# Five edits to the instruction order of a hybrid decoder layer: ffn1's last differences, a pair sum, residual loads, the memory's keys and the end of attention

## The chip, the cores and the metric

The kernel runs on one core of one Trainium2 chip. The metric is the device time of one execution in microseconds (us); before the change it is 2645.61 us, the median of 3 runs (2640.96 to 2645.98). The core's engines work side by side, each through its own queue in order: TensorE (PE: matmuls, with PEld for its weight loads), VectorE (DVE), ScalarE (ACT), GpSimd (POOL) and SyncE (SP). SP, POOL and ACT issue DMAs from their queues too.

## What is computed

One decoder layer over 1024 tokens of width 1024, all in float32, cut to its frame:

```python
def swiglu(h, w_gu, w_down):
    g, u = jnp.split(h @ w_gu, 2, axis=-1)          # D_FF = 2816
    return (jax.nn.silu(g) * u) @ w_down

f = swiglu(rmsnorm(h, ffn1_pre_g), ffn1_w_gu, ffn1_w_down)
h = h + 0.5 * rmsnorm(f, ffn1_post_g)
m = hybrid_mixer(rmsnorm(h, mix_pre_g), ...)        # stick-breaking attention | Mamba-2 SSD, then @ w_out
h = h + rmsnorm(m, mix_post_g)
c = memory_cross_attention(rmsnorm(h, xa_pre_g), rmsnorm(mem, mem_g), wq, wkv, wo)   # 256 memory rows
h = h + rmsnorm(c, xa_post_g)
f = swiglu(rmsnorm(h, ffn2_pre_g), ffn2_w_gu, ffn2_w_down)
return h + 0.5 * rmsnorm(f, ffn2_post_g)
```

## The kernel before

**Precision.** Every product of float32 values is made of three matmuls in a rounded float32 format: `split` (L263 to L269) casts a tile to its high part on ACT (L266) and subtracts that on DVE to get the low part (L268); `mm3` then multiplies high by high, high by low and low by high. A "product" below is 12 matmuls of 128x512, or 24 for a whole depth of 1024. In names, `xh` and `xl`, `whi` and `wlo`, `ath` and `atl`, `ohi` and `olo` are such pairs of parts.

**Order.** PE's instructions are chained in the order in which the program writes them. A planner's clock (`self.clock`, in planned nanoseconds of PE) counts their costs, and work for the other engines is put into `self.later` with a due time: `at(t, f)` runs `f` when the clock has passed `t`, so that its instructions are written between the matmuls of that moment. `run_later(inf)` runs all that is left at once. `urgent()` gives an instruction a higher priority, so that it may stand ahead of others on its engine. `merge(a, ta, b, tb)` runs two generators beside each other so that each has used the same share of its planned time `ta` or `tb`. On each engine the result is one queue; what stands in it behind a waiting instruction waits too.

**The first feed-forward (ffn1).** Its up projection (`up_phase` with `begin`) computes a few tiles plainly for both token halves, and the others with seven products in place of eight (`seven`, L786): a 2 by 2 block scheme, in which the two token halves and the two halves of the depth form the blocks of the activations, and sums and differences of blocks are multiplied with sums and differences of weight blocks. `S[1]`, `S[4]`, `S[5]`, `B11`, `B12`, `B21`, `B22` are such activation blocks of four tiles (k = 0 to 3) in high and low part. `B12` holds the differences gain x b - d of the second half's tiles b and d. `again(k)` (L717) loads b and d by POOL's queue, `scale` (L677) multiplies d by its gain on ACT, and `last(k)` (L720) makes the difference on DVE (L690) and splits it. `below(k)` (L711) does the same for `B21`. `homes` (L841) names the tiles in which b and d lie: the tiles `braw`, `rpost` and `dg`, `acc0` and `acc1` for k = 0 to 2; k = 3 uses a `blk`, a buffer of the weight blocks. The weight blocks themselves are made by POOL (`wc`, L741) and split into `whi`/`wlo` or `blk`.

In `seven`, a = x B22 is copied to SBUF by ACT (L795), b = x B21 likewise (L799), POOL subtracts (L800), DVE adds the product c of S[1] (L805, the tile `e`), then that of S[4] (L809); the bank of a then takes the product by B12 on top, and that of c, freed by L805, the product by S[5].

**The second feed-forward (ffn2)** does the same with `begin` false. Behind each odd tile, `pair_sums` (L637) forms sums of two tiles (`cb`, L643 on DVE), which ACT's queue stores (L645) for the down projection.

**The residual.** `resid(hh, step, start)` (L376) puts eight loads on POOL's queue, `step` apart. In the first down projection, `finish` (L949) calls it at m == 3, and at m == 4 calls `run_later(inf)`.

**Keys of the memory** (`keys`, L1479): eight products of 24 matmuls of 128x256; DVE evicts each into `sq0` (L1491), `split` puts pairs into a tile `Bt`, and SP stores a pair (L1498). DVE's additions into `yacc` (L1454) belong to the state-space branch.

**The end of attention.** `units(p)` makes the scores of head pair p (sigmoid on ACT, L1746, a scan on DVE, L1750), transposes them and multiplies them with the values; a head's sum goes to a mix tensor in DRAM through POOL (L1767). The last pair's work, `tail`, is merged with `beside`: the first output products (`mix_first`, six of eight output tiles) and the values of the memory (`memory_values`, eight products of 24 matmuls of 128x256, evicted into `ev`, transposed, split into `vo` and stored by SP, L1866). Then `mix_out` loads the mix tensors: SP loads a row into one of four buffers `oraw` (L1946), ACT squares it (L1938, L1941) and casts it (L273), DVE adds the square to `asum` (L1942) and makes the low part (L275); PE needs `asum` for the norm in the midst of the first output products.

Of the kernel before, what the change touches and what calls it, by code (L numbers as in the profile page):

```python
# [47 lines left out]
class Kern:  # L48
# [512 lines left out]
    def up_phase(self, sp, sp2, wgu, gpre, act_d, bank, load, plain, sizes, rw=None, begin=None):  # L561
# [75 lines left out]
        def pair_sums(f, even, odd):  # L637

            (t0, t1), (u0, u1) = even, odd
            j, c = f // 2, self.clock  # L640
# [6 lines left out]
            def fresh(n, a, b, op):  # L647
                combine(n, self.t(ftp, [P, H], F32, "cb", bufs=3), a, b, op)

            fresh("s6", t1, t0, ALU.subtract)  # L650
# [25 lines left out]
        def scale(x, d):  # L676
            self.kp(nc.scalar.activation(x, x, AF.Copy, scale=self.par(gpre, d)))  # L677
# [42 lines left out]
        def last(k):  # L720
            b, d = tmp["bd", k]
            if not begin:
                scale(d, k + 4)
            combine(B12[k], b, k, d, ALU.subtract)

        def at(t, f, *args):
            self.later.append((t, lambda: f(*args)))
# [114 lines left out]
        if begin:  # L842
            for k, x in enumerate((
                [(rw, "braw", 2)] * 2, [(rw, "rpost"), (self.tp, "dg")], [(rw, "acc0"), (rw, "acc1")],
            )):
                homes["ca", k] = homes["bd", k] = x
# [17 lines left out]
        if begin:  # L864
# [10 lines left out]
            for hh in range(2):  # L875
                if hh:
                    for k in range(4):
                        at(self.clock + 500 + 3000 * k, below, k)
                        if k < 3:
                            at(self.clock + 3000 + 3000 * k, again, k)  # L880
                            at(self.clock + 12000 + 1000 * k, lambda k=k: scale(tmp["bd", k][1], k + 4))
# [25 lines left out]
        for k in range(4):  # L907

            if k == 3 and begin:
                at(self.clock + 200, again, k)  # L910
                at(self.clock + 3500, lambda: scale(tmp["bd", 3][1], 7))
            at(self.clock + (1200 * k if begin else 1500 * k + 500), last, k)
# [20 lines left out]
    def down1(self, sp, wdn, act_d, xs_d, gpost, gnext):  # L933
# [15 lines left out]
        def finish(m, i):  # L949
            if m == 3:  # L950
# [3 lines left out]
                self.resid(0, 2000, 16000)  # L954
# [234 lines left out]
    def ssd(self, close):  # L1189

        nc, ap = self.nc, self.ap
        with self.tc.tile_pool(name=self.nm("ssa"), bufs=1, reuse_waits="tile") as ep, \
# [286 lines left out]
            def keys(n0, n1):  # L1479
# [6 lines left out]
                for n in range(n0, n1):  # L1486
# [4 lines left out]
                    nc.vector.tensor_tensor(out=t, in0=ps, in1=rm, op=ALU.mult)  # L1491
                    i = n % 2
                    if i == 0:
                        env["ko"] = self.t(sp, [P, 4, MEM], F32R, "Bt")
                    o = env["ko"]
                    self.split(o[:, i, :], o[:, 2 + i, :], t)
                    if i == 1:
                        nc.sync.dma_start(out=self.kv_d[n // 2][0].bitcast(F32), in_=o.bitcast(F32))  # L1498
# [78 lines left out]
    def attention(self):  # L1577
        nc, ap = self.nc, self.ap
        with self.pools("at", ["o", "a"], ["w"]) as (op, sp, wsp, pp):
# [310 lines left out]
            self.merge(tail(), 26000, beside(), 21000 + 5200 * MIXED)  # L1890
# [470 lines left out]
```

## Time and profile before

| | us |
|---|---|
| median of 3 runs | 2645.61 |
| the runs | 2640.96, 2645.61, 2645.98 |
| the profiled execution | 2636.52 |
| its span, first to last instruction | 2634.7 |
| PE busy | 2587.8 |
| mean granted PE clock | 0.994 |

The profile is of one execution. A row of the timeline gives the start, the duration, the engine with the line and the operation, output<-input, and in brackets the idle time before it and who ended it. A matmul of 128x512 in a row of them is shown with 0.39 us, but the next starts 0.23 us after it: they are pipelined. A row with x12 stands for twelve.

### The profile page before, as it was taken

How to read it: one execution, taken by the hardware profiler on the slowest of the kernel's cores; microseconds unless marked ns; L12 is line 12 of the kernel's file. 1: busy time of each engine (PE TensorE's matmuls, PEld its weight loads, DVE VectorE, ACT ScalarE, POOL GpSimd, SP SyncE). 2: the span in 40 equal slices, each digit the busy share in tenths (PEclk: the TensorE clock that was granted, in tenths of full speed). 3: DMA queues.
4: the chain of work that ended last, by engine and by line, in shares of the span. 5: the costliest groups of instructions: out<-in, count | busy, mean ns of one | idle time of the engine just before them, and what ended most of it. 6: DMA issues, size and time to landing. Idle time of an engine off the chain costs nothing. (4 is left out here: it accounts for less than half of the span.)

```text
span 2634.7 us, 36858 instructions
## 1 busy us (share of the span) xinstructions
PE 2587.8 (98%) x12850; PEld 2155.5 (82%) x12850; DVE 1981.6 (75%) x3044; ACT 1292.3 (49%) x2300; POOL 599.4 (23%) x713
## 2 busy tenths in 40 slices
PE   9899999999999999999999999999999999999999
PEld 7688888778777778888888897888878788888887
DVE  6778887778779775777777777767556888777777
ACT  7434444545356563555555555345544433333553
POOL 2555553110100000111111110101011555452000
PEclk9999999999999999999999999999999999999999
DMA  6558888875655226655555556547558453326554
GB/s 221 170 183 286 278 272 292 279 246 182 240 184 177 81 73 196 173 149 148 141 147 132 170 153 229 192 149 249 197 185 295 140 176 116 100 97 227 188 171 152
DMA packets 212970, 489.82 MB, mean 186 GB/s; under 512 B 26544, under 2 KB 35120, under 8 KB 212784
## 3 DMA queue, kind: packets, MB, share of 16 engines
q1 hardware_dynamic: 163472, 371.58, 42.8%
q0 software_dynamic: 25984, 73.42, 9.2%
q10 hardware_dynamic: 23328, 42.48, 4.3%
q8 instruction: 101, 1.65, 0.3%
q14 instruction: 85, 0.70, 0.1%
HBM read 327.46 MB, written 138.94 MB: 177 GB/s over the span
## 5 line engine op out<-in xcount | busy, mean ns | idle before, releaser
L139 PE MATMUL mm<-xh,whi 128*128 128x512 f32 x1320 | 522.6, 405 | 7.4 <-ACT xh L273 3.0
L139 PE MATMUL mm<-xl,whi 128*128 128x512 f32 (+1 forms) x1252 | 488.1, 390 | 4.7 <-DVE xl L268 4.4
L139 PE MATMUL mm<-xh,wlo 128*128 128x512 f32 x1272 | 489.0, 392 | 0.0
L139 PEld LDWEIGHTS mm<-xh,whi 128*128 128x128 f32 x1320 | 249.1, 189 | 50.3 <-ACT xh L266 3.9
L139 PEld LDWEIGHTS mm<-xh,wlo 128*128 128x128 f32 x1272 | 238.9, 188 | 52.0 <-DVE wlo L268 0.2
L139 PEld LDWEIGHTS mm<-xl,whi 128*128 128x128 f32 x1252 | 236.6, 189 | 39.3 <-DVE xl L268 6.3
L1750 DVE TENSOR_TENSOR_SCAN nb<-nb,begin 128x128 f32<-128x128 f32 (+7 forms) x128 | 171.5, 1352 | 52.4 <-ACT nb L1746 51.9
L1746 ACT ACTIVATE nb<-z,scale 128x128 f32<-128x128 f32 (+2 forms) x192 | 107.7, 580 | 77.8 <-PE z L139 77.5
L268 DVE TENSOR_TENSOR wlo<-wraw,whi 128x1024 fp32r<-128x1024 f32 x70 | 85.4, 1221 | 54.8 <-ACT whi L266 51.4
L266 ACT CAST whi<-wraw 128x1024 fp32r<-128x1024 f32 (+1 forms) x87 | 83.8, 964 | 79.2 <-PE mm L139 55.2
L1767 POOL DMA_DIRECT2D mix<-sq x64 | 52.9, 826 | 229.1 <-DVE sq L1765 131.0
L658 ACT ACTIVATE ft<-ft 128x512 f32<-128x512 f32 x88 | 55.5, 632 | 98.1 <-DVE ft L657 96.1
L139 PE MATMUL dn<-xh,wlo 128*128 128x512 f32 x296 | 101.3, 390 | 0.0
L741 POOL TENSOR_TENSOR wc<-wraw,raw 128x512 f32<-128x512 f32 x56 | 80.3, 1433 | 64.7 <-DVE whi L268 17.8
L741 POOL TENSOR_TENSOR wc<-raw,wraw 128x512 f32<-128x512 f32 x55 | 81.1, 1474 | 51.0 <-DVE blk L268 21.6
L268 DVE TENSOR_TENSOR atl<-tr,ath 128x512 fp32r<-128x512 f32 (+1 forms) x108 | 67.9, 632 | 29.9 <-ACT ath L266 29.5
L826 POOL TENSOR_TENSOR ft<-ft,e 128x512 f32<-128x512 f32 x37 | 59.7, 1613 | 121.1 <-DVE e L825 45.1
L139 PE MATMUL mm<-ath,v 128*128 128x256 f32 x320 | 86.1, 292 | 0.1
L266 ACT CAST ath<-tr 128x512 fp32r<-128x512 f32 (+1 forms) x108 | 58.8, 546 | 55.5 <-PE tr L142 50.9
L139 PE MATMUL dn<-xh,blk 128*128 128x512 f32 x264 | 85.2, 389 | 0.0
L266 ACT CAST wlo<-wc 128x512 fp32r<-128x512 f32 x79 | 49.1, 621 | 71.0 <-PE dn L139 26.1
L139 PE MATMUL mm<-atl,v 128*128 128x256 f32 x320 | 83.1, 282 | 0.7 <-DVE atl L268 0.7
(566 smaller groups left out, 6799.7 us busy)
## 6 DMA issues: line engine op xcount, KB each, us to landing
whi<-dwhi SPq DMA_DIRECT2D x82, 512.0 KB, 3.6
wlo<-dwlo SPq DMA_DIRECT2D x82, 512.0 KB, 4.7
wraw<-in_w_gu SPq DMA_DIRECT2D x43, 512.0 KB, 4.1
raw<-in_w_gu SPq DMA_DIRECT2D x37, 512.0 KB, 4.2
dwhi<-bh SPq DMA_DIRECT2D x66, 256.0 KB, 4.1
dwlo<-bl SPq DMA_DIRECT2D x66, 256.0 KB, 4.3
wraw<-xs SPq DMA_DIRECT2D x56, 256.0 KB, 3.1
xs<-ft ACTq DMA_DIRECT2D x54, 256.0 KB, 3.3
```

Of the source, the lines that this page charges most:

```text
L139: self._pe(self.nc.tensor.matmul(out, lhsT, rhs, start=start, stop=stop, skip_group_check=self.more), cost)
L266: self.kp(self.nc.scalar.copy(hi, src))
L268: self.nc.vector.tensor_tensor(out=lo, in0=src, in1=hi.bitcast(F32), op=ALU.subtract)
L658: nc.scalar.activation(t, t, AF.Silu)
L741: nc.gpsimd.tensor_tensor(out=t, in0=a, in1=b, op=op)
L826: nc.gpsimd.tensor_tensor(out=t1, in0=t1, in1=e, op=ALU.mult)
L1746: nc.scalar.activation(nb[:, s0:s1], z[:, 0:n], AF.Sigmoid, scale=sc[:, i : i + 1])
L1750: nc.vector.tensor_tensor_scan(out=nb[:, 0:Wd][:, ::-1], data0=nb[:, 0:Wd][:, ::-1], data1=begin[:, S - Wd : S][:, ::-1], initial=0.0, op0 ...
L1767: nc.gpsimd.dma_start(out=self.mix_d[p][a * 64 : a * 64 + 64, csl], in_=o, accum_op=ALU.add)
```

## The change

Five places are edited, and nothing that is computed changes.

1. ffn1's last differences. k = 3 gets two `cb` tiles as its home. `below` is due every 2200 instead of every 3000, `again` now for all four k in the plain products, and `scale` 5000 after it. A new function `differ` makes the difference in place 1000 later, and `last` with `begin` only splits it, every 800.
2. ffn2's first pair sum: with f == 5 all its steps are due 4000 later, the first one too, which was written at once.
3. The residual's eight loads of the first half are due 3500 apart instead of 2000.
4. The memory's keys: the eviction is `urgent`, the last pair lies in a tile `csr`, and POOL stores the pairs instead of SP.
5. The end of attention: `tail` is merged with a planned time of 32500 instead of 26000.

```diff
         def pair_sums(f, even, odd):
             (t0, t1), (u0, u1) = even, odd
-            j, c = f // 2, self.clock
+            j, c = f // 2, self.clock + (4000 if f == 5 and not begin else 0)
...
-            fresh("s6", t1, t0, ALU.subtract)
+            if c == self.clock:
+                fresh("s6", t1, t0, ALU.subtract)
+            else:
+                at(c, fresh, "s6", t1, t0, ALU.subtract)
...
         def last(k):
             b, d = tmp["bd", k]
-            if not begin:
-                scale(d, k + 4)
+            if begin:
+                self.split(*B12[k], b)
+                return
+            scale(d, k + 4)
             combine(B12[k], b, k, d, ALU.subtract)
+
+        def differ(k):
+            b, d = tmp["bd", k]
+            self.kp(
+                nc.vector.scalar_tensor_tensor(
+                    out=b, in0=b, scalar=self.par(gpre, k), in1=d, op0=ALU.mult, op1=ALU.subtract
+                )
+            )
...
-                [(rw, "braw", 2)] * 2, [(rw, "rpost"), (self.tp, "dg")], [(rw, "acc0"), (rw, "acc1")],
+                [(rw, "braw", 2)] * 2, [(rw, "rpost"), (self.tp, "dg")], [(rw, "acc0"), (rw, "acc1")], [(ftp, "cb", 3)] * 2,
...
-                        at(self.clock + 500 + 3000 * k, below, k)
-                        if k < 3:
-                            at(self.clock + 3000 + 3000 * k, again, k)
-                            at(self.clock + 12000 + 1000 * k, lambda k=k: scale(tmp["bd", k][1], k + 4))
+                        at(self.clock + 500 + 2200 * k, below, k)
+                        at(self.clock + 2000 + 2200 * k, again, k)
+                        at(self.clock + 7000 + 2200 * k, lambda k=k: scale(tmp["bd", k][1], k + 4))
+                        at(self.clock + 8000 + 2200 * k, differ, k)
...
-            if k == 3 and begin:
-                at(self.clock + 200, again, k)
-                at(self.clock + 3500, lambda: scale(tmp["bd", 3][1], 7))
-            at(self.clock + (1200 * k if begin else 1500 * k + 500), last, k)
+            at(self.clock + (800 * k if begin else 1500 * k + 500), last, k)
...
-                self.resid(0, 2000, 16000)
+                self.resid(0, 3500, 16000)
...
-                    nc.vector.tensor_tensor(out=t, in0=ps, in1=rm, op=ALU.mult)
+                    with self.urgent():
+                        nc.vector.tensor_tensor(out=t, in0=ps, in1=rm, op=ALU.mult)
...
-                        env["ko"] = self.t(sp, [P, 4, MEM], F32R, "Bt")
+                        env["ko"] = self.t(sp, [P, 4, MEM], F32R, "Bt" if n < 6 else "csr")
...
-                        nc.sync.dma_start(out=self.kv_d[n // 2][0].bitcast(F32), in_=o.bitcast(F32))
+                        nc.gpsimd.dma_start(out=self.kv_d[n // 2][0].bitcast(F32), in_=o.bitcast(F32))
...
-            self.merge(tail(), 26000, beside(), 21000 + 5200 * MIXED)
+            self.merge(tail(), 32500, beside(), 21000 + 5200 * MIXED)
```

The change adds lines, so that a line of the changed kernel has a number 3 to 14 higher (L690 becomes L693, L805 becomes L818, L1491 becomes L1502, L1946 becomes L1957). No engine gets more or fewer computing instructions; the four stores of the keys go from SP's queue to POOL's. Between the end of ffn1's first seven-product pass and the memory's keys the queues of both programs are the same, row for row, and with them the eight residual loads of edit 3.

How the order moves, at three places. First DVE's queue where ffn1's seven-product passes begin. `bl` and `bh` (before) and the named homes (after) are the differences, `xl_28` to `xl_31` the low parts of `B12` for k = 0 to 3; `wlo`, `whi` and `blk` rows are low parts of weight blocks. Before:

```order
L690 SCALAR_TENSOR_TENSOR bl_958<-braw_830,params_78,braw_831 128x512
L268 TENSOR_TENSOR wlo_988<-wc_986,wlo_988 128x512
L268 TENSOR_TENSOR blk_1014<-wc_1012,blk_1014 128x512
L268 TENSOR_TENSOR xl_28_104<-bl_958,xh_12_88 128x512
L690 SCALAR_TENSOR_TENSOR bh_970<-rpost_873,params_78,dg_874 128x512
L268 TENSOR_TENSOR blk_1033<-wc_1031,blk_1033 128x512
L268 TENSOR_TENSOR whi_1074<-wc_1072,whi_1074 128x512
L268 TENSOR_TENSOR xl_29_105<-bh_970,xh_13_89 128x512
L690 SCALAR_TENSOR_TENSOR bl_980<-acc_270_895,params_78,acc_271_896 128x512
L690 SCALAR_TENSOR_TENSOR bh_997<-blk_962,params_78 128x512
L268 TENSOR_TENSOR wlo_1095<-wc_1093,wlo_1095 128x512
L268 TENSOR_TENSOR xl_30_106<-bl_980,xh_14_90 128x512
```

And now:

```order
L734 SCALAR_TENSOR_TENSOR cb_904<-cb_904,params_78,cb_905 128x512
L268 TENSOR_TENSOR whi_964<-wraw_854,whi_964 128x512
L268 TENSOR_TENSOR xl_28_104<-braw_826,xh_12_88 128x512
L268 TENSOR_TENSOR xl_29_105<-rpost_846,xh_13_89 128x512
L268 TENSOR_TENSOR xl_30_106<-acc_271_884,xh_14_90 128x512
L268 TENSOR_TENSOR xl_31_107<-cb_904,xh_15_91 128x512
L268 TENSOR_TENSOR wlo_991<-wc_989,wlo_991 128x512
L268 TENSOR_TENSOR blk_1012<-wc_1010,blk_1012 128x512
L268 TENSOR_TENSOR blk_1031<-wc_1029,blk_1031 128x512
L268 TENSOR_TENSOR blk_1051<-wraw_871,blk_1051 128x512
L268 TENSOR_TENSOR whi_1072<-wc_1070,whi_1072 128x512
L818 TENSOR_TENSOR e_184<-sq_282_962,dn_1009 128x512
```

The four low parts now follow each other, with the differences ahead of them, and L818 (before: L805, the row behind the last one shown) has six weight halves and those four in front. On ACT the four casts `xh_12` to `xh_15` likewise follow each other, ahead of the copy at L795, which stood behind the first of them.

Second, DVE's queue at the memory's keys: `wlo` low parts of the key weights, `Bt` of the keys, `sq_2149` and now `sq_2147` the eviction of the fourth key tile. Before:

```order
L268 TENSOR_TENSOR wlo_9688<-wraw_9685,whi_9687 128x1024
L268 TENSOR_TENSOR Bt_9577<-sq_2138_9575,Bt_9577 128x256
L1454 TENSOR_TENSOR yacc_2031_9101<-yacc_2031_9101,sq_2145_9614 128x512
L1454 TENSOR_TENSOR yacc_2031_9101<-yacc_2031_9101,sq_2146_9619 128x512
L268 TENSOR_TENSOR wlo_9724<-wraw_9721,whi_9723 128x1024
L1454 TENSOR_TENSOR yacc_2032_9102<-yacc_2032_9102,sq_2147_9624 128x512
L1454 TENSOR_TENSOR yacc_2032_9102<-yacc_2032_9102,sq_2148_9629 128x512
L1491 TENSOR_TENSOR sq_2149_9644<-mm_9586,Ct_9206 128x256
```

And now:

```order
L268 TENSOR_TENSOR Bt_9575<-sq_2136_9573,Bt_9575 128x256
L268 TENSOR_TENSOR wlo_9686<-wraw_9683,whi_9685 128x1024
L1464 TENSOR_TENSOR yacc_2029_9099<-yacc_2029_9099,sq_2143_9612 128x512
L1464 TENSOR_TENSOR yacc_2029_9099<-yacc_2029_9099,sq_2144_9617 128x512
L268 TENSOR_TENSOR wlo_9722<-wraw_9719,whi_9721 128x1024
L1464 TENSOR_TENSOR yacc_2030_9100<-yacc_2030_9100,sq_2145_9622 128x512
L1502 TENSOR_TENSOR sq_2147_9642<-mm_9584,Ct_9204 128x256
L1464 TENSOR_TENSOR yacc_2030_9100<-yacc_2030_9100,sq_2146_9627 128x512
```

The eviction has passed one addition, and the low part of the third key tile one weight's.

Third, SP's queue at the end of attention: `kv<-vo` are the stores of the memory's values, `oraw<-mix` the loads of the mix rows, `whi<-dwhi` and `wlo<-dwlo` the weights of an output tile. Before:

```order
L1866 DMA kv_127<-vo_15840 512x1x128
L182 DMA wlo_16051<-dwlo_9830 128x1024
L185 DMA wraw_16141<-in_w_out 128x1024
L1866 DMA kv_129<-vo_15904 512x1x128
L1946 DMA oraw_15975<-mix_130 128x512
L1946 DMA oraw_15983<-mix_131 128x512
L1946 DMA oraw_15992<-mix_132 128x512
L1946 DMA oraw_16001<-mix_133 128x512
L1866 DMA kv_129<-vo_15942 512x1x128
L1946 DMA oraw_16010<-mix_134 128x512
```

And now:

```order
L182 DMA whi_16044<-dwhi_9825 128x1024
L1877 DMA kv_127<-vo_15859 512x1x128
L182 DMA wlo_16045<-dwlo_9826 128x1024
L182 DMA whi_16048<-dwhi_9827 128x1024
L1877 DMA kv_127<-vo_15899 512x1x128
L182 DMA wlo_16049<-dwlo_9828 128x1024
L1957 DMA oraw_15973<-mix_130 128x512
L1957 DMA oraw_15981<-mix_131 128x512
L1877 DMA kv_129<-vo_15933 512x1x128
L1957 DMA oraw_15990<-mix_132 128x512
L1877 DMA kv_129<-vo_15940 512x1x128
L1957 DMA oraw_15999<-mix_133 128x512
```

The first loads have passed a value store, the fourth has fallen behind the last one, and the weights of the seventh output tile (`whi_16044`, `wlo_16045`) stand between the value stores. On ACT the square of the fifth mix row, which stood behind the casts of the sixth and seventh, now stands ahead of them.

## The prediction

> **What bounds the kernel now.** The first part of the profile's page comes first:
>
> ```profile
> PE 2587.8 (98%) x12850; PEld 2155.5 (82%) x12850; DVE 1981.6 (75%) x3044; ACT 1292.3 (49%) x2300; POOL 599.4 (23%) x713
> ```
>
> TensorE (PE) is busy for 2587.8 of 2634.7 us. The change leaves its instructions as many as they were, so all there is to win is the 47 us in which it stands still, and the time lost to a lowered clock. Next the waits of PE: engine, line, what was waited for, then us in total, times, longest.
>
> ```profile
> PE dn L139 <- ACT F L1069: 4.6, 1, 4.6
> PE mm L139 <- DVE xl L268: 4.4, 3, 1.7
> PE mm L139 <- DVE e L805: 3.4, 2, 3.2
> PE mm L139 <- ACT xh L266: 2.7, 2, 1.6
> PE ms L139 <- DVE asum L1942: 2.0, 1, 2.0
> PE mm L139 <- DVE sq L1491: 1.9, 1, 1.9
> ```
>
> All but the first (4.6 us in the first down projection) name lines that the change touches. Last, the stretches around them: us, busy time and instructions of PE, PEld, DVE, ACT and POOL, granted clock, DMA share, GB/s.
>
> ```profile
> 87.00:109.00 22.00, 14.85 (x47) 9.69 (x45) 19.38 (x22) 10.95 (x19) 11.52 (x8) 0.77 0.28 103
> 484.00:492.00 8.00, 5.03 (x21) 3.50 (x20) 8.00 (x14) 6.27 (x12) 0.75 (x2) 1.00 0.61 197
> 1014.00:1023.00 9.00, 7.07 (x47) 6.89 (x47) 4.92 (x9) 3.12 (x5) 0.94 (x1) 0.81 0.50 180
> 1490.00:1577.00 87.00, 86.09 (x574) 78.39 (x575) 69.04 (x98) 47.02 (x90) 10.58 (x27) 1.00 0.51 156
> 1575.00:1606.00 31.00, 27.53 (x118) 21.79 (x117) 20.86 (x32) 18.22 (x30) 6.05 (x10) 0.94 0.81 269
> 2090.00:2105.00 15.00, 11.80 (x46) 9.25 (x45) 10.85 (x14) 5.94 (x11) 9.10 (x7) 0.89 0.31 105
> ```
>
> A stall here costs more than its own length: the granted clock falls behind it. In 1014 to 1023 it is 0.81, so 9 x 0.19 = 1.7 us; in 1575 to 1606 31 x 0.06 = 1.9 us; in 2090 to 2105 15 x 0.11 = 1.7 us. The stretch 484 to 492 is PE idle for 3 us at clock 1.00, so not every stall is followed by this. I price a stall of about 2 us or more at 1.6 us on top, one of 1.2 us or less at nothing.
>
> The Trainium skill, page "TensorE: Matmul & The Clock Gate", section "HAM oscillation — how this bites in real kernels", sums its rule up as "no PE-idle gaps >~3.4µs". The stretch 1014 to 1023 has less than 2 us of idle time and still loses clock, so the trace speaks against the rule as a limit; what would follow from it is the third rival.
>
> **Part 1, the last differences of ffn1.** PE where ffn1's plain products end and its seven-product passes begin: start, duration, what it is, idle time before it and who ended it.
>
> ```profile
> 89.02 2.88 PE L139 MATMUL dn<-S,wlo 128*128 128x512 f32 x12
> 93.61 0.51 PE L139 MATMUL mm<-xl,whi 128*128 128x512 f32 x1 [1.24 <-DVE xl L268]
> 105.44 3.72 PE L139 MATMUL dn<-S,wlo 128*128 128x512 f32 x12
> 109.00 0.40 PE L139 MATMUL mm<-xh,blk 128*128 128x512 f32 x1
> ```
>
> A product of 12 matmuls issues in 2.73 us. The product by B12 starts 2.85 us after 89.02, at 91.87, and the next only at 105.44: 13.57 us, and that one takes 3.56 at the lowered clock. Together 17.13 instead of 5.46, a loss of 11.7 us. Why:
>
> ```profile
> 87.53 0.72 ACT L677 ACTIVATE acc<-acc,params 128x512 f32<-128x512 f32 x1 [1.91 <-DMA acc<-in_xT]
> 91.23 0.58 ACT L795 COPY sq<-mm 128x512 f32<-128x512 f32 x1
> 90.59 0.69 DVE L268 TENSOR_TENSOR wlo<-wc,wlo 128x512 fp32r<-128x512 f32 x1
> 91.79 1.76 DVE L268 TENSOR_TENSOR xl<-bl,xh 128x512 fp32r<-128x512 f32 x1
> 102.59 0.68 DVE L805 TENSOR_TENSOR e<-sq,dn 128x512 f32<-128x512 f32 x1
> ```
>
> Per k, VectorE (DVE) makes a difference, ScalarE (ACT) casts it, DVE makes the low part; POOL's weight sums run beside it, and a DVE operation that takes 0.69 us alone takes 1.76 beside them. The change puts the four differences ahead, so that four casts and four low parts are left. In the new order the four casts stand before the copy at L795, which frees B12's PSUM bank: raw data land as before (87.5), two scales, one weight cast and four casts at 0.5 to 0.7 us each follow, one more weight cast and the copy: about 93.4. B12 starts then, and not at 91.87. The next product waits for L805, which now stands behind the four low parts and six weight halves: eleven DVE operations from about 90.3. From 90.59 to 102.59 the row above and L805's enclose twelve operations, 1.0 us each with POOL at work; eleven such give 90.3 + 11 = 101.3 for L805's end. At 0.6 us each it would be 97, with the fast rate of the row at 90.59; at 1.5 us, between the two rows, 106.8, no gain. I take 101.1 for the start against 105.44: 4.3 us. The stall ahead of that product stays (some 4 us), so it loses 1.6 us to the clock by the price above, and 0.83 (3.56 less 2.73) now: 0.8 more. **3.5 us, between 0 and 8.**
>
> **Part 2, ffn2's first pair sum.**
>
> ```profile
> 2093.66 1.76 DVE L643 TENSOR_TENSOR cb<-ft,ft 128x512 f32<-128x512 f32 x1 [1.19 <-POOL ft L826]
> 2095.82 0.59 ACT L799 COPY sq<-dn 128x512 f32<-128x512 f32 x1 [3.04 <-DVE cb L643]
> 2099.09 0.69 DVE L805 TENSOR_TENSOR e<-sq,mm 128x512 f32<-128x512 f32 x1 [1.15 <-POOL sq L800]
> 2099.83 4.61 PE L139 MATMUL mm<-S,whi 128*128 128x512 f32 x12 [3.20 <-DVE e L805]
> ```
>
> ACT's store of the sum, at the head of its queue, waits 3.04 us for L643; the copy L799 is behind it, then POOL's L800, then L805, then PE. Moved 4000 back, the sum comes after two more weight casts and the store leaves the copy's way: L799 about 2.4 us earlier. POOL then takes a weight sum (1.3 us) before L800, and L805 ends near 2098.6: 1.1 us earlier. A stall of 2.1 us is left; whether the clock falls is even: 1.1 + 0.8 = **1.9 us, between 0.5 and 4.9** (all 3.2 and 1.7). What waits later is the pair sum itself; its readers are in the down projection.
>
> **Part 3, the residual's loads.** No row of any engine moves: the callbacks are flushed together at m == 4 in both programs. **0 us.** Nothing hides this edit; it does nothing, so there is no cover to lose.
>
> **Part 4, the memory's keys.**
>
> ```profile
> 1015.51 1.48 DVE L1454 TENSOR_TENSOR yacc<-yacc,sq 128x512 f32<-128x512 f32 x2
> 1016.90 0.42 DVE L1491 TENSOR_TENSOR sq<-mm,Ct 128x256 f32<-128x256 f32 x1
> kv<-Bt SPq DMA_DIRECT2D x4, 512.0 KB, 3.7
> h<-F POOLq DMA_DIRECT2D x36, 256.0 KB, 2.8
> dwhi<-bh POOLq DMA_DIRECT2D x4, 256.0 KB, 6.4
> ```
>
> PE waits 1.9 us for the eviction at 1016.90, which two additions of 0.7 us hold up; now one does: the stall falls to 1.2 us, and with it the fall of the clock should go: 0.7 + 1.6 = 2.3 us. Against it: the second pair's cast must wait for the first store, now on POOL, and stands ahead of a weight cast on ACT. POOL's stores land in 2.8 to 6.4 us, SP's in 3.7. A landing as soon as now costs nothing; one 2.7 us later holds up two casts and, behind them on DVE, the eviction, past 1016.90 again. **2.3 us, between -0.3 and 3.5 (the whole stall and its clock).**
>
> The Trainium skill, page "DMA: Bandwidth & Descriptors", section "Latency and other measured facts", gives the first byte of a hardware queue as about 600 ns and of POOL's as about 1 us. That makes the moved store 0.4 us later, an estimate from that page, and the cast still on time; no run here shows that figure by itself.
>
> **Part 5, the end of attention.** Head pair 7 now advances faster beside the output products and memory values, and is done some 2.3 memory-value products early. Today:
>
> ```profile
> 1576.65 2.37 SPq L1946 DMA_DIRECT2D oraw<-mix  x4
> 1590.78 0.72 ACT L273 ACTIVATE ohi<-oraw,params 128x512 fp32r<-128x512 f32 x1 [2.15 <-DMA oraw<-mix]
> 1592.79 0.62 ACT L1941 ACTIVATE sq<-oraw 128x512 f32<-128x512 f32 x1
> 1593.43 4.92 SPq L1946 DMA_DIRECT2D oraw<-mix  x3
> 1596.71 0.50 PE L139 MATMUL dn<-olo,whi 128*128 128x512 f32 x1 [0.67 <-DVE olo L275]
> 1600.81 1.02 PE L139 MATMUL ms<-small,asum 128*128 128x1 f32 x8 [1.98 <-DVE asum L1942]
> ```
>
> Four buffers carry the mix rows. The fifth's square (1592.79) stands behind the casts of the sixth and seventh, which wait 2.15 us and more for their DMA; its end lets the ninth load go (1593.43), and the last squares stand behind that. In the new order the fifth's square comes before those casts, and the first load goes about 1.5 us sooner, but the fourth stands behind the last value store and goes later. Going through it load by load with 3 to 5 us per load, the sum is ready between 0.9 us before PE's need and 1.2 after it, instead of 2: 1.5 us of the two waits (2.65 us), and the fall of the clock behind them (1.6). Against it: wlo of the seventh output tile now stands behind the fifth value store and can be 0.5 us late. **3.1 us, between -1.0 (the sum no sooner, both loads later) and 4.6 (the waits and 1.9 of clock).**
>
> **Sum.** 3.5 + 1.9 + 0 + 2.3 + 3.1 = 10.8 us. The profiled execution took 2636.5 us (its span and 1.8 around it), so it would take 2625.7. It stands 9.1 us under the median of the runs, 2645.6; the same 10.8 us off that give **2634.8 us**.
>
> **Rivals.** (a) The stalls only change their names, chance 0.16. Speaking for it: part 1 puts its casts ahead of L795, part 2 a weight sum ahead of L800, and the fourth mix load goes later. Against it: at each place the row that is waited for does come sooner in the new order. A gain of 0 + 0.5 - 0.3 + 1.5 = 1.7 us: 2643.9.
>
> (b) Slower, 0.09: VectorE becomes the bound of the denser tail. DVE's groups from 1490 to 1577 (times, then busy us and mean ns):
>
> ```profile
> L1750 DVE TENSOR_TENSOR_SCAN nb<-nb,begin 128x384 f32<-128x384 f32 (+7 forms) x14 | 20.5, 1467 | 4.1 <-ACT nb L1746 3.9
> L268 DVE TENSOR_TENSOR atl<-tr,ath 128x512 fp32r<-128x512 f32 (+1 forms) x17 | 10.9, 640 | 3.9 <-ACT ath L266 3.9
> L1765 DVE TENSOR_TENSOR sq<-sq 64x256 f32<-64x256 f32 x9 | 3.7, 416 | 1.0 <-ACT sq L1764 0.8
> ```
>
> These 35 of DVE's 69 us are attention's. At the new rate, 32500 against 26000, they fall in 87 x 26/32.5 = 70 us: 35/70 + 34/87 = 0.89 of the engine instead of 0.79. If the engine's slack is too small from there, each of the pair's eight units gives PE a stall of 1.2 us (what one addition now leaves in part 4), and the clock falls twice: 9.6 + 3.2 = 12.8 us, against 7.7 from parts 1, 2 and 4: 2650.7. Against it: in that stretch PE stands still for under 1 us of 87.
>
> (c) The clock does not come back, 0.12: where a fall has other causes than the stall, only idle time is won: 4.3 - 0.8 + 1.1 + 0.7 + 1.5 = 6.8 us, 2638.8. For it speaks the stretch 484 to 492, where a stall and a fall do not go together. By the Trainium skill's rule on 3.4 us, quoted above, this is the case that holds.
>
> (d) Everything named goes, clock included, 0.11: 8 + 4.9 + 3.5 + 4.6 = 21.0 us, 2624.6. For it speaks only that all five upper bounds are read from rows; against it, the new order leaves a producer ahead of each wait.
>
> The forecast itself has 0.52. Its own range is 2630 to 2640. About 0.2%, 5.3 us, is what a measurement of this kernel can tell from no change. Faster by more than that: the forecast, (c) and (d), 0.75; within it (a), 0.16; slower (b), 0.09. The range takes in (a) and (d) and leaves out most of (b): 2623 to 2647.
>
> **What would show it.** Part 1: the B12 product as one block starting 1.5 us later than now, the next at about 101. Part 2: under 2.2 us before L805's product. Part 4: one addition ahead of the fourth eviction, clock near 1.00 in that stretch. Part 5: no wait over 1.2 us for asum. PE's idle time should fall from 47 to about 40 us. I am wrong if new waits stand in the attention tail, with releasers that are scans or low parts; if the ffn1 product waits for L795 or L805 past 105; or if the gaps shrink and the clock does not rise.

## The result, and the profile after

The changed kernel is as fast as the kernel before:

| | before | changed |
|---|---|---|
| median of 20 runs, us | 2640.83 (2637.46 to 2645.98) | 2640.53 (2637.10 to 2647.03) |
| ratio, with its 95% interval | | 0.9999 [0.9992, 1.0006] |
| span of the profiled execution, us | 2634.7 | 2636.9 |

The three runs that the prediction counted from lay 4.8 us above the median of twenty. Against the forecast of 10.8 us off stand 0.3 us, give or take 1.8.

Busy times of the changed kernel, as in the first part of the page before:

```profile
PE 2586.9 (98%) x12850; PEld 2153.9 (82%) x12850; DVE 1981.5 (75%) x3044; ACT 1293.0 (49%) x2300; POOL 601.8 (23%) x717
```

PE stands still for 2636.9 - 2586.9 = 50.0 us; it was 46.9, and about 40 were forecast. Its waits (engine, line, what was waited for; us in total, times, longest):

```profile
PE dn L139 <- DVE e L818: 5.9, 2, 5.6
...
PE mm L139 <- DVE e L818: 3.1, 2, 2.8
...
PE ms L139 <- DVE atl L268: 2.6, 1, 2.6
...
PE dn L139 <- ACT ohi L273: 2.0, 1, 2.0
PE dn L139 <- DMA wlo<-dwlo: 2.0, 1, 2.0
PE mm L139 <- DMA wlo<-dwlo: 1.9, 1, 1.9
...
PE ms L139 <- DVE asum L1953: 1.4, 1, 1.4
```

The small waits of ffn1 have become one of 5.6 us. The keys' eviction has left the head of the list (0.8 us instead of 1.9), and the longest wait by the pair sum (L818, before L805, in the second feed-forward) is 2.8 us instead of 3.2. Four waits of 1.9 to 2.6 us are new, all of them from 1530 to 1670, at the end of attention and behind it. The stretches of the prediction, in the changed kernel (us; busy time and instructions of PE, PEld, DVE, ACT, POOL; granted clock, DMA share, GB/s). It reaches the keys 4.5 us sooner than the kernel before and the end of attention 8 us sooner, so these two stretches are taken that much earlier, to hold about the same work; the first down projection comes 2.6 us sooner, too, and its stall (481.9 to 484.6) now lies ahead of the second row:

```profile
87.00:109.00 22.00, 16.42 (x60) 12.68 (x59) 19.54 (x24) 11.21 (x20) 14.62 (x11) 0.84 0.31 109
484.00:492.00 8.00, 7.37 (x25) 5.98 (x26) 8.00 (x15) 5.90 (x13) 1.57 (x3) 0.79 0.44 140
...
1009.50:1018.50 9.00, 8.18 (x70) 8.00 (x69) 3.95 (x8) 1.49 (x4) 1.50 (x2) 1.00 0.67 233
1482.00:1569.00 87.00, 82.58 (x545) 75.22 (x546) 67.01 (x97) 46.38 (x91) 11.43 (x28) 1.00 0.47 131
...
1575.00:1606.00 31.00, 27.01 (x114) 21.10 (x113) 21.55 (x32) 19.24 (x29) 3.79 (x7) 0.94 0.84 292
2090.00:2105.00 15.00, 12.16 (x49) 9.63 (x49) 12.80 (x13) 4.91 (x9) 10.31 (x8) 0.92 0.29 107
```

Part 4 did what was forecast: the keys' stretch has 0.8 us of idle time left, was idle for 1.9, and its clock is 1.00 instead of 0.81. The attention tail lost: PE is busy for 82.58 of 87 us, and was for 86.09, with DVE no busier than before (67.01 against 69.04).

All traces have 12850 matmuls in the same order outside the tail, so one can read how long PE takes from a given matmul to a later one. The stages: ffn1's change of passes (from 87 us), the first down projection (470), the memory's keys (1003), the end of attention with the first part of the output projection (1480), its second pass (1618), and the second feed-forward's pass (2052). Of the edits, number 1 is ffn1's differences, 2 the pair sum, 3 the residual's step, 4 the keys, 5 the number 32500 for the end of attention. "Row" is the memory's rms row made early, as explained below. One profiled execution each, us, taken from the starts of the same matmuls:

| kernel: its edits | ffn1 | down 1 | keys | tail | pass 2 | ffn2 |
|---|---|---|---|---|---|---|
| before | 93.4 | 124.2 | 72.1 | 138.0 | 80.7 | 141.6 |
| e6: 3 | 92.9 | 123.2 | 72.2 | 138.4 | 81.8 | 142.1 |
| e4: 4 | 93.0 | 125.5 | 69.5 | 138.9 | 82.4 | 141.9 |
| e3: 1 | 91.5 | 127.5 | 72.1 | 141.6 | 84.4 | 141.7 |
| e1: 1 2 3 4 | 91.3 | 127.6 | 69.5 | 143.4 | 85.8 | 141.7 |
| e2: 5 | 92.9 | 123.3 | 70.7 | 145.7 | 82.6 | 141.7 |
| changed: 1 2 3 4 5 | 90.8 | 123.3 | 69.6 | 144.9 | 84.4 | 141.3 |
| e7: all, value stores on POOL | 90.3 | 127.4 | 69.3 | 145.8 | 84.4 | 141.2 |
| e8: all, row | 90.1 | 125.4 | 69.4 | 142.4 | 84.3 | 141.3 |
| e9: all, row, value stores on POOL | 91.2 | 125.2 | 69.9 | 143.0 | 83.1 | 141.3 |
| e10: all, row, mix rows on POOL | 91.7 | 126.3 | 69.9 | 142.2 | 86.0 | 141.3 |
| e11: all, row, residual on SP | 91.0 | 125.3 | 69.5 | 140.0 | 82.1 | 141.3 |
| e12: 1 2 3 4, row | 91.9 | 124.9 | 70.0 | 141.7 | 80.7 | 141.6 |
| e13: 1 2 3 4, row, residual on SP | 91.0 | 127.1 | 69.5 | 139.0 | 82.5 | 142.4 |

In ffn1, the kernels with edit 1 need 90.1 to 91.9, those without it 92.9 to 93.4; in the keys 69.3 to 70.0 with edit 4, 70.7 to 72.2 without. The tail has 144.9 to 145.8 with edit 5 and the late row, and 138.0 to 143.4 in all others, without edit 5 or with the early row. "Down 1" and "pass 2", which no edit was written for, scatter by 4.4 and 5.3 us; ffn2, with edit 2 in some of the kernels, by 1.2.

### The profile page after: what moved, and what is told of

Read it like the earlier page. It is cut to its first block, busy times and chain, and to the rows that moved or that the text cites. A ratio compares the mean times of both kernels' runs of the same rounds, so it can differ in the third digit from the quotient of the medians.

```text
span 2636.9 us, 36866 instructions
## 1 busy us (share of the span) xinstructions
PE 2586.9 (98%) x12850; PEld 2153.9 (82%) x12850; DVE 1981.5 (75%) x3044; ACT 1293.0 (49%) x2300; POOL 601.8 (23%) x717
## 3 DMA queue, kind: packets, MB, share of 16 engines
q8 instruction: 101, 1.65, 0.3%
## 5 line engine op out<-in xcount | busy, mean ns | idle before, releaser
L266 ACT CAST whi<-wc 128x512 fp32r<-128x512 f32 x80 | 49.7, 621 | 71.1 <-PE dn L139 25.9
L139 PE MATMUL dn<-xh,whi 128*128 128x512 f32 x240 | 83.9, 394 | 0.0
```

The costliest lines, as they stand in the source:

```text
L139: self._pe(self.nc.tensor.matmul(out, lhsT, rhs, start=start, stop=stop, skip_group_check=self.more), cost)
L266: self.kp(self.nc.scalar.copy(hi, src))
```

## The experiments

**Which edit gives, which takes.** Four kernels: the changed one with the end of attention put back (e1), and edits 5, 1 and 4 each alone in the kernel before (e2, e3, e4).

```diff
 e1, in the changed kernel:
-            self.merge(tail(), 32500, beside(), 21000 + 5200 * MIXED)
+            self.merge(tail(), 26000, beside(), 21000 + 5200 * MIXED)
 e2, in the kernel before:
-            self.merge(tail(), 26000, beside(), 21000 + 5200 * MIXED)
+            self.merge(tail(), 32500, beside(), 21000 + 5200 * MIXED)
```

e3 takes from the change only the hunks on `last`, `differ`, `homes` and their due times; e4 only those on `keys`.

> All edits but the fifth: the tail is merged with 26000 again. Theory A (the end of attention gives back what the others win): matched by their order, PE's matmuls run 7.1 us earlier after the keys with the change, and 2.6 later after the first output products; so with the tail as before the kernel should be 5 to 7 us faster than before, ratio 0.9973 to 0.9981, and PE's waits for atl (2.6) and for wlo's DMA (1.9) in the tail should be gone. Theory B (single executions differ by chance by up to 10 us, and no edit is worth more than 1 us): ratio 0.9995 to 1.0005.

> The fifth edit alone: the tail merged with 32500. Theory A: 4 to 10 us slower than before, ratio 1.0015 to 1.0038, with PE waits for atl, a weight's DMA and ohi in the end of attention. Theory B: ratio 0.9995 to 1.0005.

> The first edit alone. Theory A: 2.6 us faster, ratio 0.9990 (one PE wait of 5.6 us for L818 in place of the five by the B12 product). Theory C (what ffn1 wins is given back in the down projection's waits for F and the clock behind them, as a fall of 1 us at 484 in the changed kernel's profile suggests): ratio 0.9996 to 1.0000. Theory B: 0.9995 to 1.0005.

> The fourth edit alone. Theory A: 2.6 us faster, ratio 0.9990, with the stall ahead of the fourth key's eviction at 0.8 us instead of 1.9 and the granted clock at 1.00 behind it. Theory B: ratio 0.9995 to 1.0005.

| kernel | median, us | ratio to before |
|---|---|---|
| e1: all but edit 5 | 2636.92 | 0.9990 [0.9980, 1.0000] |
| e2: edit 5 alone | 2645.30 | 1.0019 [1.0010, 1.0027] |
| e3: edit 1 alone | 2637.80 | 0.9993 [0.9984, 1.0002] |
| e4: edit 4 alone | 2637.66 | 0.9993 [0.9985, 1.0002] |

Edit 5 by itself makes the kernel slower, by 5.0 us (2.6 to 7.1), and without it the rest is a gain of 2.6 us at the edge of what can be told. The two single gains of 1.8 us have intervals that reach 1. So theory A, that the end of attention gives back what the other edits win, holds by its sign and by the waits: e2 lies inside its range, and in e1 the wait for atl at `ms` is 0.3 us again and that for wlo is gone. Its sizes were too large: 5 to 7 us were expected of e1, and 2.6 of each of the two single edits. That it is all chance does not hold, by e2's interval; whether ffn1's gain is lost in the first down projection can't be told from e3's time. In e2 the waits of the changed kernel's tail come again where nothing else was changed (waits of PE):

```profile
PE ms L139 <- DVE atl L268: 2.6, 1, 2.6
...
PE dn L139 <- ACT ohi L273: 1.8, 1, 1.8
...
PE dn L139 <- DMA wlo<-dwlo: 1.6, 1, 1.6
...
PE ms L139 <- DVE asum L1942: 1.3, 1, 1.3
...
PE mm L139 <- DMA wlo<-dwlo: 1.2, 1, 1.2
```

**Where the 2.6 us come from.** DVE and PE of the changed kernel around that wait (start, duration, engine, line, operation, output<-input, idle time before it and who ended it):

```profile
1531.17 3.14 DVE L1761 TENSOR_TENSOR_SCAN nb<-nb,begin 128x640 f32<-128x640 f32 x2 [1.65 <-ACT nb L1757]
1534.22 0.67 DVE L1932 TENSOR_TENSOR sq<-mm,rpre 128x512 f32<-128x512 f32 x1
1534.81 1.21 DVE L268 TENSOR_TENSOR wlo<-wraw,whi 128x1024 fp32r<-128x1024 f32 x1
1535.94 0.68 DVE L268 TENSOR_TENSOR atl<-ms,ath 128x512 fp32r<-128x512 f32 x1
...
1533.03 0.60 PE L142 MATMUL ms<-ident,nb 128*128 128x128 f32 x4
1533.95 0.58 ACT L266 CAST ath<-ms 128x512 fp32r<-128x512 f32 x1
1536.68 0.71 PE L139 MATMUL ms<-ident,cmem 128*128 128x128 f32 x4 [2.57 <-DVE atl L268]
```

Every third group of attention's transposes is put into the PSUM bank `ms` (1533.03). The low part atl frees it, and stands on DVE behind two scans, a mix sum and a weight's low part; 1.4 us of these are left when its cast ath is done at 1534.53. The memory's rms row wants the same bank right behind those transposes and is the one to wait, with all of PE behind it. In the kernel before, the same product follows without a wait:

```profile
1533.29 0.60 PE L142 MATMUL ms<-ident,nb 128*128 128x128 f32 x4
1534.54 0.69 DVE L268 TENSOR_TENSOR atl<-ms,ath 128x512 fp32r<-128x512 f32 x1 [2.23 <-ACT ath L266]
1535.89 0.61 PE L139 MATMUL ms<-ident,cmem 128*128 128x128 f32 x4
```

Counted from the start of the transposes, atl ends after 1.94 us before and after 3.59 now, and PE reaches the row's product after 2.60 before and would after 1.08 now. So the wait has two halves: the bank comes free 1.65 us later, and the tighter merge asks for it 1.5 us sooner.

The row depends on the memory alone, so it can be made earlier, during the seventh head pair's projections (e8). The tiles dg and sq1 change places for it. From e8's diff:

```diff
+                if n == 7:
+                    mem_r.append(self.t(self.tp, [P, H], F32, "dg")[:, 0:MEM])
+                    self.rms_rows(self.mem_c[:, :], mem_r[0])
...
-                rm = self.t(self.tp, [P, H], F32, "sq1")[:, 0:MEM]
-                self.rms_rows(self.mem_c[:, :], rm)
-                yield
+                rm = mem_r[0]
```

e7 puts the value stores (L1877) on POOL's queue (`nc.gpsimd` in place of `nc.sync`), e9 does both, and e6 is a control: the kernel before with 3500 for the residual.

> A control: the kernel before with only the residual's number at 3500. Its queues hold the same instructions in the same order as the kernel before, so every theory expects a ratio of 1.0000, and what it differs from that is what five rounds cannot tell apart. If the small gains of the two single edits (0.9993 each) are real and not the spread of such a comparison, this one must lie within 0.0004 of 1.

> The changed kernel with the stores of the memory's values on POOL's DMA queue instead of SP's. Theory A (the end of attention loses by waits that have names: here the value stores that stand ahead of the mix weights' and the mix rows' loads on SP): the wait of 1.9 us for wlo near 1573 goes and the 2.0 us for ohi near 1593 shrinks, together 2 to 4 us, ratio to the kernel before 0.9985 to 0.9992. Rival B (the loads are late by the DMA engines' own load, not by the queue's order): wlo still lands 6 to 7 us after its issue and the wait stays over 1 us, ratio 0.9996 to 1.0002. Rival C (VectorE is what holds the stretch): the waits take another name, ratio 0.9996 to 1.0002, and the stretch 1490 to 1612 stays as long as the changed kernel's.

> The changed kernel with the memory's rms row made during the seventh head pair's projections, so that its product no longer waits for the PSUM bank that an attention tile of the tail holds. Theory A: the wait of 2.57 us ahead of the product of ident and cmem goes, and nothing takes its place: 2.5 us less, ratio to the kernel before about 0.9990. Rival C (VectorE is late anyway): the first value's products or the attention's transposes wait for VectorE within the next 10 us instead, at least 1.5 of the 2.57 us come back, ratio 0.9995 to 1.0002.

> Both of these in the changed kernel: the memory's rms row early and the value stores on POOL's queue. Theory A: the losses are separate and add, 4.5 to 6.5 us less than the changed kernel, ratio to the kernel before 0.9975 to 0.9983, and the end of attention then costs no more than in the kernel before. Rival C: under 2 us less, ratio 0.9993 or more.

| kernel | median, us | ratio to before |
|---|---|---|
| e6: edit 3 alone | 2638.99 | 0.9999 [0.9989, 1.0008] |
| e7: all, value stores on POOL | 2641.26 | 0.9997 [0.9988, 1.0006] |
| e8: all, row | 2636.32 | 0.9985 [0.9976, 0.9993] |
| e9: all, row, value stores on POOL | 2637.22 | 0.9992 [0.9984, 1.0001] |

The control says what such a comparison leaves open: about 0.1% to either side. The early row gains: the wait is gone in e8, the tail falls from 145.5 (the mean of the three kernels with edit 5 and the late row) to 142.4 us, and the time is 0.15% under the kernel before, where the changed kernel alone is level with it. Theory A holds for this wait, but not its "nothing takes its place". Near 1483 PE waits 2.2 to 2.9 us for DVE's xl in all six kernels with the early row, against 0.7 to 2.1 in the eight others, and the granted clock falls there in all six, in one of the eight. Behind it, in e8, are two loads of ev that take 5.3 us to land, in place of 3.8 in the changed kernel; why is not shown. So the early row as it was built gives part of its gain back.

For the stores theory A falls. In e7 the wait for wlo near 1573 went, and others grew (waits of PE from 1480 to 1612, changed kernel and then e7):

```profile
PE ms L139 <- DVE atl L268: 2.6, 1, 2.6
PE dn L139 <- ACT ohi L273: 2.0, 1, 2.0
PE mm L139 <- DMA wlo<-dwlo: 1.9, 1, 1.9
...
PE ms L139 <- DVE asum L1953: 1.4, 1, 1.4
PE z L139 <- ACT nb L1757: 1.2, 2, 1.0
```

```profile
PE ms L139 <- DVE atl L268: 2.6, 1, 2.6
PE ms L139 <- DVE asum L1953: 2.2, 1, 2.2
PE z L139 <- ACT nb L1757: 1.9, 2, 1.7
PE dn L139 <- DVE olo L275: 1.6, 2, 0.9
...
PE mm L139 <- DMA wlo<-dwlo: 0.3, 1, 0.3
```

The order on SP's queue decides which transfer is late, not how late all of them are. That fits one half of rival B, and the other half, a wait for wlo of over 1 us, did not come (0.3). The two transfers of wlo that were issued in this stretch of the changed kernel (1560 to 1580; operation, count, KB each, median us from issue to landing) landed as slowly with the stores ahead of them as in e7 (1560 to 1590) without, and slower than the 4.9 us that all 82 of the changed kernel have as their median:

```profile
wlo<-dwlo SPq DMA_DIRECT2D x2, 512.0 KB, 7.3
```

```profile
wlo<-dwlo SPq DMA_DIRECT2D x2, 512.0 KB, 7.9
```

Rival C's signs came: other names, and a tail as long as the changed kernel's (145.8 against 144.9). Its cause did not. DVE's asum and olo, which PE waits for in e7, wait for ACT, and ACT for the load of a mix row, as in the changed kernel (3.09 us there):

```profile
1594.08 0.72 ACT L273 ACTIVATE ohi<-oraw,params 128x512 fp32r<-128x512 f32 x1 [3.16 <-DMA oraw<-mix]
```

In e9 the two do not add: 0.9992, where theory A had 0.9975 to 0.9983 and the early row alone measures 0.9985.

**Order or load.** With the early row kept: the mix rows' loads (oraw) on POOL's queue (e10), or the residual's eight loads of 256 KB on SP's queue between the mix rows, in place of POOL's, which sends them all at 1580 to 1585 (e11). e12 is e8 with 26000.

```diff
 e10:
-                nc.sync.dma_start(out=raw, in_=self.mix_d[kt][:, hh * H : (hh + 1) * H])
+                nc.gpsimd.dma_start(out=raw, in_=self.mix_d[kt][:, hh * H : (hh + 1) * H])
 e11, with resid() taking the queue:
-            self.resid(0, 5000, 12000)
+            self.resid(0, 5000, 12000, nc.sync)
```

> The changed kernel with the early rms row, and with the loads of the mix rows (oraw) on POOL's DMA queue instead of SP's, so that weights and mix rows no longer stand behind one another. Theory A (order on SP makes wlo and oraw late): the waits for wlo near 1573 (1.1 us) and ohi near 1592 (1.8 us) go, 2 to 3 us less than with the early row alone, ratio to the kernel before 0.9974 to 0.9978. Rival B (the DMA engines are full there): the waits change size by under 0.7 us in sum or move to the residual's loads, ratio 0.9981 to 0.9989, as the early row alone.

> The changed kernel with the early rms row, and with the eight loads of the residual that POOL issues at 1580 to 1585 put on SP's queue between the mix rows instead, so that they come after the mix rows that are wanted first. Rival B (the DMA engines are full: 2 MB of residual go out at the same time as the mix rows): the wait for ohi near 1592 falls from 1.8 us to under 0.8, and with it the clock's fall near 1595 may go, 1 to 3.5 us less than with the early row alone, ratio 0.9972 to 0.9981. Theory A (order on the queue): the residual's loads now stand ahead of weights on SP, the wait for ohi stays or a weight is late, ratio 0.9985 to 0.9995.

> The changed kernel with the number of the end of attention back at 26000 and with the early rms row. At 26000 no stall stands ahead of the memory's row. Theory A (the early row gains only what the number 32500 had lost): nothing over the changed kernel with 26000 alone, ratio to the kernel before 0.9988 to 0.9994. Rival D (the early row is a gain by itself, by shorter queues on VectorE and ScalarE in the tail): 2 to 4 us under that, ratio 0.9975 to 0.9983. If edits 1, 2 and 4 are worth 2.5 us and the rest is noise, this and the changed kernel with the early row alone agree within 1 us, and the edit to 32500 is worth nothing even when its stall is taken away.

| kernel | median, us | ratio to before |
|---|---|---|
| e10: all, row, mix rows on POOL | 2639.89 | 1.0001 [0.9993, 1.0010] |
| e11: all, row, residual on SP | 2636.30 | 0.9986 [0.9977, 0.9995] |
| e12: 1 2 3 4, row | 2635.24 | 0.9987 [0.9978, 0.9996] |

e10 missed both expectations: its median is 3.6 us over e8's. The mix rows now come sooner and the weight later (the first row is e10's wait near 1576; in e8 it was 1.1 us):

```profile
PE mm L139 <- DMA wlo<-dwlo: 3.0, 1, 3.0
PE mm L139 <- DVE xl L1931: 2.5, 1, 2.5
PE z L139 <- ACT nb L1760: 1.3, 2, 1.1
PE ms L139 <- DVE asum L1955: 0.7, 1, 0.7
```

The wait for ohi, 1.8 us in e8, went. In sum PE waits about as long in both profiles (7.7 us in e8, 8.1 in e10), and the tail takes 142.2 us against 142.4, so where e10 loses its time is not shown.

e11 took the wait for ohi away and let that for asum grow from under 0.2 to 2.3 us; its time is e8's. e12 misses rival D and answers what edit 5 is worth once its stall is gone: nothing. With the early row, 26000 and 32500 agree within 1.1 us, less than such a comparison can tell. That e12 is better than e1 by the row itself is not shown (0.9987 against 0.9990).

**A version that beats both.** e11 with 26000:

> The changed kernel with the number of the end of attention back at 26000, the early rms row and the residual's loads on SP's queue: a candidate that should beat both. If the residual's loads take DMA time from the mix rows (rival B, which the last look at the waits half bears out: the wait for ohi went, the wait for asum grew), it is 0.5 to 2 us under the same kernel with the loads on POOL, ratio 0.9979 to 0.9985. If the DMA engines are full either way and only the order of landings changes, it equals it: 0.9985 to 0.9990.

2631.81 us (six runs), ratio 0.9965 [0.9953, 0.9978]: 9.2 us under the kernel before by the ratio, 8.2 by the medians, more than either theory gave it. From 1580 to 1612, e12 and then e13:

```profile
1580.00:1612.00 32.00, 29.26 (x127) 23.27 (x126) 25.01 (x37) 22.25 (x34) 3.79 (x7) 0.95 0.75 263
```

```profile
1580.00:1612.00 32.00, 30.76 (x143) 25.15 (x142) 27.42 (x41) 23.52 (x36) 0.00 (x0) 1.00 0.78 262
```

There the clock stays at 1.00, and 143 matmuls get through in place of 127: those that e12 issues in these 32 us take e13 28.3. The wait for asum is 0.9 us in e13 (1.6 in e12). Ahead of 1490, near the wait for xl, e13 loses 0.7 us more to the clock. That accounts for the 2.7 us of the tail (141.7 to 139.0); why the median gains more than that is open.

## What the prediction had right and wrong, point by point

The forecast was 10.8 us faster, and the result is no change: 0.3 us. The time, 2640.5, lies inside the range of 2623 to 2647, but the likeliest case behind it failed, at part 5. What each part measured: 2.0 + 0.4 + 0 + 2.2 - 5.0 = -0.4 us, in place of 3.5 + 1.9 + 0 + 2.3 + 3.1; parts 1, 2 and 4 by single traces, part 5 by e2's median. That gain and loss cancel so nearly is chance. So is that the time missed by only 5.7 us: the gain missed by 10.5, and the three runs counted from lay 4.8 too high.

By its time rival (a), the stalls only change their names, comes nearest (2643.9). By its terms it did not come: two stalls shrank, and part 5 lost. That is the shape of rival (b), where parts 1, 2 and 4 win 7.7 us (4.6 came) and the tail loses 12.8 (5.0 came). The list of waits with which the prediction opens leaves out three rows of the view without a mark, of 3.0, 3.0 and 2.2 us, at lines that the change does not touch; so less of PE's idle time was to be won than "all but the first" says.

**Part 5 is the step that failed.** "The sum is ready between 0.9 us before PE's need and 1.2 after it, instead of 2" was near: the wait for asum fell from 2.0 to 1.4 us. But the part went through the mix rows' loads, where the old stall stood, and took nothing else of the denser tail into its sum than "wlo of the seventh output tile ... can be 0.5 us late". That wait was 1.9 us, the one for ohi 2.0, and the bank `ms` cost 2.6, which is in no step at all. In place of +3.1 us, inside bounds of -1.0 and 4.6, edit 5 alone measured -5.0 (-7.1 to -2.6); by e1, without it, against the changed kernel it is some -2.4. One of the prediction's own signs of being wrong came: a new wait in the tail whose releaser is a low part. Rival (b) had the right place and sign with the wrong mechanism: VectorE did not become the bound; it got no busier. What counted was a bank that two streams share, asked for 1.5 us sooner by PE and freed 1.65 us later by DVE. With the row out of its way (e8) edit 5 costs nothing that can be told, and gains nothing either (e12): the 3.1 us are nowhere.

**Part 1 was mis-sized.** The product was to start at 101.1:

```profile
91.86 0.50 PE L139 MATMUL mm<-xh,whi 128*128 128x512 f32 x1
...
100.50 5.48 PE L139 MATMUL dn<-S,wlo 128*128 128x512 f32 x12 [5.58 <-DVE e L818]
...
99.77 0.68 DVE L818 TENSOR_TENSOR e<-sq,dn 128x512 f32<-128x512 f32 x1
```

It started at 100.50, and B12's product at 91.86 instead of the 93.4 forecast. But the wait was one piece of 5.58 us instead of "some 4" (the step's own times, 93.4 + 2.73 to 101.1, give 5.0), and all twelve matmuls behind it ran at the low clock, 5.48 us, where the step had 3.56 and a share of the 1.6. Ten traces with the edit and four without differ by 2.0 us in that stage (91.1 against 93.0 on average), not 3.5, but inside its bounds of 0 and 8; by time e3 alone gives 1.8, with an interval that reaches 1. And the first down projection may take it back: it needs 126.0 us on average with the edit and 124.1 without. There PE waits for DVE's L1041, and that stands behind a product that waits for a weight from memory (e3, DVE and then PE):

```profile
548.91 0.69 DVE L1019 TENSOR_TENSOR cb<-wraw,xl 128x512 f32<-128x512 f32 x1 [2.71 <-DMA wraw<-in_w_dn]
...
552.53 0.68 DVE L1041 TENSOR_TENSOR ft<-dn,F 128x512 f32<-128x512 f32 x1
...
553.89 1.65 PE L139 MATMUL dn<-hl,whi 128*128 128x512 f32 x3 [7.97 <-ACT F L1076]
```

A wait that a transfer ends need not get shorter when PE comes sooner. The changed kernel itself lost nothing there (123.3), and the column scatters by 4.4 us, so this stays open.

**Part 2 was mis-sized.** "POOL then takes a weight sum (1.3 us) before L800" was two of them, at 1.7 us each, beside DVE operations of 1.8 us, the pair sum among them (changed kernel):

```profile
2096.24 3.42 POOL L754 TENSOR_TENSOR wc<-raw 128x512 f32<-128x512 f32 x2
2099.63 1.71 POOL L813 TENSOR_TENSOR sq<-sq,sq 128x512 f32<-128x512 f32 x1
...
2098.45 1.76 DVE L643 TENSOR_TENSOR cb<-ft,ft 128x512 f32<-128x512 f32 x1
```

The copy's gain of over 2 us was spent on that, and the stall fell from 3.2 to 2.8 us, not 2.1: 0.4 us, just outside the part's lower bound of 0.5. The edit was not run alone.

**Part 3 was right**: 0 us, and e6 measured 0.9999 [0.9989, 1.0008].

**Part 4 was right.** The stall is 0.8 us instead of 1.9 (1.2 were forecast) and the clock does not fall: 2.2 us on average between the traces with and without the edit, forecast 2.3. By time, e4 alone gives 1.8 us with an interval that reaches 1. The stores on POOL's queue cost nothing that shows.

**The price of a stall was wrong as a rule.** "A stall of about 2 us or more at 1.6 us on top" holds on average at best. The same stall of 2.57 us at `ms` cost nothing in the changed kernel and a fall in e7 and e2. From 1530 to 1545, changed kernel, then e7:

```profile
1530.00:1545.00 15.00, 12.22 (x86) 11.08 (x85) 10.23 (x11) 8.50 (x15) 1.17 (x3) 1.00 0.18 40
```

```profile
1530.00:1545.00 15.00, 12.22 (x67) 10.73 (x66) 10.24 (x12) 5.96 (x12) 0.34 (x2) 0.89 0.21 70
```

PE is busy for 12.22 us of 15 in both, and 0.11 x 15 = 1.7 us are lost in one of them alone. The stall at 484 that the prediction saw stay without a fall (2.7 us) has one behind it in the changed kernel, at the same length. What decides it is in the last section.

## What to carry to other kernels

When a change makes two streams of work overlap more tightly, list every buffer and bank that both use, and for each ask what its reader stands behind on its own engine; the old stall's neighbourhood is not the whole of it. Where a transfer is late in a stretch whose DMA engines are busy for 0.8 of the time, another order of the queue may only pick another victim, as in e7; look for the transfers that aren't needed yet, as in e13. And before a price is put on a stall, compare two executions: if the same stall costs something in one and nothing in the other, it has a chance and not a price.

## What the runs showed of the hardware

The low clock comes in pieces of one length and on a grid. In each trace the granted clock is 1 or 0.5, and up to the last matmul the stretches at 0.5 last 3.41, 6.83 or 10.24 us, that is one, two or three times 3.413. Starts in the kernel before, us from the start of the span, with the distance to the one before in units of 3.4133 us:

```
start     96.9   550.8   670.3  1018.5  1602.2  2100.5
distance          133.0    35.0   102.0   171.0   146.0
```

Whether a stall of 2 to 3 us is followed by such a piece depends on where it lies on the grid, which differs from one execution to the next. In all 14 traces, 70 grid pieces at full clock have PE idle for 1.93 us or more, and each of them is followed by a piece at half clock; of the 56 with 1.32 to 1.92 us 19 are, and of some ten thousand with less a single one. The stall of 2.57 us at `ms` has 1.92 us in one piece in the changed kernel, and no fall; it has 2.43 in e7 and 2.26 in e2, and a fall. That of 2.7 us at 484 is cut into 1.46 and 1.27 in the kernel before, and lies in one piece in the changed kernel.

Up to the last matmul the profiled execution of the kernel before has 9 such pieces, of the changed one 7, of e2 7, and of e3 and e1 13: at half of 3.41 us each, up to 10 us between executions, about as much as the runs of one kernel spread (8.5 us for the kernel before). So one profiled execution cannot rank two kernels that are 0.1% apart: e1 and e3 were profiled 8 us over the kernel before, and their medians lie under it.

The Trainium skill, page "TensorE: Matmul & The Clock Gate", Part 1, has this rule: the gate watches activity in a window of 4096 cycles, 3413 ns, which runs freely and doesn't start with the kernel. The distances above agree with it. The same page's "no PE-idle gaps >~3.4µs", which the prediction cited, is not a limit that protects: gaps of 1.9 to 2.9 us were followed by falls here.
